# Part of a depthwise convolution moved from VectorE to ScalarE copies and GpSimd additions, in a two-layer hybrid block

## The chip, the core and the metric

The kernel runs on one core of a Trainium2 chip. The metric is the device time of one execution in microseconds, taken as the median over runs. The core has TensorE (PE in the profile, with its weight loads as PEld), VectorE (DVE), ScalarE (ACT), GpSimd (POOL) and SyncE (SP), which issues all DMAs here. Each engine works off its own instructions in order; the engines wait for each other by semaphores.

## The reference

Two layers of a block over 1024 latent tokens and 256 context tokens of width 1024. Each layer projects the normalised input into ten groups of columns and feeds three branches: a state-space branch (SSD) behind a convolution of 5 taps over 1280 channels, an attention branch, and a conformer branch:

```
def dwconv(x, w, b):
    pad = w.shape[0] // 2
    y = lax.conv_general_dilated(x, w[:, None, :].astype(x.dtype), ..., feature_group_count=x.shape[-1])
    return y + b.astype(x.dtype)
...
def conformer_branch(ua, ub, gate, conv_w, conv_b, ln_g, ln_b, pw_w, pw_b):
    u = ua * jax.nn.sigmoid(ub)
    u = jax.nn.silu(layernorm(dwconv(u, conv_w, conv_b), ln_g, ln_b))
    u = u @ pw_w + pw_b
    return u * jax.nn.silu(gate)
```

The conformer convolution is depthwise with 31 taps over 512 channels. The three branches are concatenated and multiplied by an output matrix; the result is gated and added to the input. In the second layer (layer 1 below) the context tokens get no output, so its convolution covers 1024 tokens and not 1280.

## The kernel before, in words

A layer has three stages that follow each other on TensorE: the projections (`phase_b`), attention with the SSD scan beside it (`attn`, `ssd`), and the output matrix (`out_half`). The program is written with a due time ahead of each group of instructions (`at(us)`); a scheduler that knows these times and a model of the engines makes from them one fixed order per engine. The order that results, and not the text of the code, is what runs.

The change lies in the second half of `phase_b`. It works through 17 blocks of 256 projected columns (`block`, numbered from 0 here). A block loads its weights as two halves, each in three steps: a DMA into a raw tile `wr` (L357, one buffer), a copy on ScalarE to the rounded part `wth`, a subtraction on GpSimd to the rest `wtl` (L359). Then come the matmuls, three for each of the eight slices of the depth (`wth` with the rounded input `hh`, `wtl` with `hh`, `wth` with the input's rest `hl`). The weight tiles have two buffers, so block i + 2 may be prepared once block i has been used. A block's output comes in groups of 512, 512 and 256 tokens of 24 matmuls each, in PSUM tiles `m` with four buffers, for each of its two halves.

Blocks 0 to 8 alternate. Even ones hold two of the ten 128-channel slices of the 5-tap convolution: ScalarE copies them into `xpad`, and `conv_x` computes `xcv` on VectorE with one tensor_scalar (L205), four scalar_tensor_tensor (L208), a tanh on ScalarE (`th`) and one more scalar_tensor_tensor. For eight of the ten slices TensorE then transposes `xcv` in three groups, and ScalarE copies those out into `xsg` (one buffer for all ten token tiles), which a single DMA stores. Odd blocks hold the gate `ub` and the value `ua` of one of four conformer slices j: VectorE forms `up` (two buffers, 15 zeros of padding written by GpSimd), and `conv_cm` computes slice j of the 31-tap convolution into `cac`, on VectorE alone: a tensor_scalar for tap 0 with the bias, then 30 scalar_tensor_tensor in place, each over 1295 elements per partition (1024 in layer 1), due 1.7 us apart (`CM_PACE`). I call these conv 0 to conv 3. Blocks 9 to 16 are gated projections (`z`, `gc`, `ga`), whose results go through ScalarE (`g_t`) and VectorE (`g_o`, two buffers) to memory.

`cm_tail` finishes the conformer branch: per token tile TensorE transposes the four `cac` slices, VectorE takes mean and variance (`bs`), normalises (`xn`), TensorE transposes back, and a small matrix product follows (`v`). Its due time is `TAIL` us after that of block 9's start, so its transposes come between the matmuls of blocks 9 to 16 in TensorE's order. A token tile's transposes need all four convolutions.

Of the kernel before, what the change touches and what calls it, by code (L numbers as in the profile page):

```python
# [10 lines left out]
AF = mybir.ActivationFunctionType  # L11
ALU = mybir.AluOpType
# [6 lines left out]
PT_ = 2  # L19
PX_ = 1  # L20
CM_PACE = 1.7
TAIL = 40.0
SSD_PACE = 25.0
AT_PACE = 1.2
VLAG = 1
# [13 lines left out]
NT = T // 128  # L39
# [121 lines left out]
def build(tc, a, out, depth=DEPTH, dump=None):  # L161
    nc = tc.nc
    es = ExitStack()
    V, S, G, P, Y = nc.vector, nc.scalar, nc.gpsimd, nc.tensor, nc.sync

    def at(us):
        tc.cur_priority = int(us * 100)

    def pool(st, name, bufs=1, **k):
        return st.enter_context(tc.tile_pool(name=name, bufs=bufs, **k))  # L170
# [3 lines left out]
    def mk(p, shape, tag, dt=F32, bufs=None):  # L174
        uid[0] += 1
        k = {} if bufs is None else {"bufs": bufs}
        return p.tile(shape, dt, tag=tag, name=f"{tag}_{uid[0]}", **k)
# [8 lines left out]
    def dr(shape, name, dt=F32):  # L186
        t = dp.tile(shape, dt, tag=name, name=name)
        if dump is not None:
            dump[name] = t
        return t  # L190
# [4 lines left out]
    def tr(o, i, idt):  # L195
        P.transpose(o, i, idt)  # L196

    def act(o, i, f, **k):
        S.activation(o, i, f, **k)  # L199

    def ts(e, o, i, s1, op0, s2=None, op1=None):
        if op1 is None:
            e.tensor_scalar(o, i, s1, None, op0)
        else:
            e.tensor_scalar(o, i, s1, s2, op0, op1)  # L205

    def stt(o, i, s, i1, op0, op1):
        V.scalar_tensor_tensor(o, i, s, i1, op0, op1)  # L208
# [24 lines left out]
    for l in range(depth):  # L233
        t = mk(cp, [128, NCOL], f"colc{l}")
        Y.dma_start(out=t, in_=a["colc"][l])
        colc.append(t)
        t = mk(cp, [128, NROW], f"rowc{l}")
# [18 lines left out]
    xt_d = dr([NT, 128, 768], "xt_d")  # L256
    bt_d = dr([NT, 128, 256], "bt_d")
# [11 lines left out]
    def rs_pow(o, i, scale, tmp, n):  # L269
        ts(V, tmp, i, scale, ALU.mult, EPS, ALU.add)  # L270
        G.tensor_tensor(o, tmp, neg[:, :n], ALU.pow)
# [38 lines left out]
    def cc(l, n, j=0, w=1):  # L310
        o = CO[n][0] + j * w
        return colc[l][:, o:o + w]
# [36 lines left out]
    def wblock(p, rp, src, tag, bufs, e=None, rtag="wr", rbufs=1):  # L349
        shape = list(src.shape)  # L350
        hi = mk(p, shape, tag + "h", F32R, bufs=bufs)
        lo = mk(p, shape, tag + "l", F32R, bufs=bufs)
        n = shape[1] // 2
        for k in range(2):
            s = slice(n * k, n * k + n)
            raw = mk(rp, [128, n, shape[2]], rtag, bufs=rbufs)
            Y.dma_start(out=raw, in_=src[:, s])  # L357
            act(hi[:, s], raw, AF.Copy)
            (e or G).tensor_tensor(lo[:, s], raw, hi[:, s].bitcast(F32), ALU.subtract)  # L359
        return hi, lo  # L360
# [73 lines left out]
    def phase_b(l, nh, b0, pp):  # L434
# [71 lines left out]
        gp = pool(st_r, f"gp{l}", side="right")  # L506
# [31 lines left out]
        up_p = pool(s2, f"up{l}")  # L538
        xp_p = pool(s2, f"xp{l}")
        cw = mk(up_p, [128, 4, 31], "cmw")  # L540
# [6 lines left out]
        NCM = 1024 if last else 1295  # L547

        def conv_cm(j, t0, pace):
            u, o = ups[j], cac[j]  # L550
            at(t0)
            ts(V, o[:, 0:NCM], u[:, 0:NCM], cw[:, j, 0:1], ALU.mult, cc(l, "cmb", j), ALU.add)
            for k in range(1, 31):
                at(t0 + k * pace)
                stt(o[:, 0:NCM], u[:, k:k + NCM], cw[:, j, k:k + 1], o[:, 0:NCM], ALU.mult, ALU.add)

        def conv_x(j, t0):
            xp = xps[j]
            at(t0)
            o = mk(xp_p, [128, 1282], "xcv", bufs=2)  # L560
            w = sw[:, 5 * j:5 * j + 5]
            ts(V, o, xp[:, 0:1282], w[:, 0:1], ALU.mult, sw[:, 50 + j:51 + j], ALU.add)
            for k in range(1, 5):
                at(t0 + 2 * k)
                stt(o, xp[:, k:k + 1282], w[:, k:k + 1], o, ALU.mult, ALU.add)
            at(t0 + 10)
            th = mk(up_p, [128, 1282], "th")
            act(th, o, AF.Tanh)
            stt(o, th, 1.0, o, ALU.add, ALU.mult)
            if j >= 6:  # L570
                d = bT_d[j - 6] if j < 8 else cT_d[j - 8]
                Y.dma_start(out=d[:, 0:1024], in_=o[:, 0:1024])
                Y.dma_start(out=d[:, 1024:1280], in_=o[:, 1026:1282])
            if j < 8:
                at(t0 + XLAG)
                sg = mk(gp, [128, NT, 128], "xsg")
                for ta in (0, 4, 8):
                    n = min(4, NT - ta)
                    ps = mk(*((pt, [128, 4, 128], "t") if ta == 4 else (px, [128, 4, 128], "x")))
                    for t in range(ta, ta + n):  # L580
                        c0 = t * 128 + (2 if t >= 8 else 0)
                        tr(ps[:, t - ta, :], o[:, c0:c0 + 128], idf)
                    act(sg[:, ta:ta + n, :], ps[:, 0:n, :], AF.Copy)
                if j < 6:
                    d = xt_d[:, :, 128 * j:128 * j + 128]
                else:
                    d = bt_d[:, :, 128 * (j - 6):128 * (j - 6) + 128]
                Y.dma_start(out=d.rearrange("t p f -> p t f"), in_=sg)

        def gate(ps, t0, n, d):  # L590
            th = mk(gp, [128, 512], "g_t", bufs=2)
# [59 lines left out]
        tlp = pool(s3, f"tl{l}")  # L651
# [4 lines left out]
        def cm_tail(c0):  # L656
            at(c0 - 10)
            pwh, pwl = wblock(tlp, wt, a["pww"][l], "pw", 1)
            hc = mk(tlp, [128, 16], "hc")
            ts(V, hc[:, 0:8], colc[l][:, CO["lng"][0]:CO["lng"][0] + 8], 0.5, ALU.mult)  # L660
            groups = [(0, 4), (4, 4)] + ([] if last else [(8, 2)])
            for tb, tn in groups:
                uh = mk(tlp, [128, 4, 512], "uh", F32R)
                ul = mk(tlp, [128, 4, 512], "ul", F32R)
                for t in range(tb, tb + tn):
                    at(c0 + 4 * t)
                    c1 = t * 128 + (15 if t >= 8 else 0)
                    ps = mk(pt, [128, 4, 128], "t")
                    for j in range(4):
                        tr(ps[:, j, :], cac[j][:, c1:c1 + 128], idf)  # L670
                    bs = mk(tlp, [128, 12], "bs", bufs=2)
                    V.bn_stats(bs[:, 0:6], ps.rearrange("p j t -> p (j t)"))
                    V.bn_aggr(bs[:, 6:8], bs[:, 0:6])
                    rs_pow(bs[:, 9:10], bs[:, 7:8], 1.0, bs[:, 8:9], 1)
                    xn = mk(gp, [128, 512], "xn", bufs=1)
                    ts(V, xn, ps.rearrange("p j t -> p (j t)"), bs[:, 6:7], ALU.subtract, bs[:, 9:10], ALU.mult)
                    ps2 = mk(px, [128, 4, 128], "x")
                    for j in range(4):
                        tr(ps2[:, j, :], xn[:, 128 * j:128 * j + 128], idf)
                    th = mk(tlp, [128, 4, 128], "lth", bufs=1)  # L680
                    v2 = mk(tlp, [128, 4, 128], "lv2", bufs=1)
                    for j in range(4):
                        g, b = hc[:, j:j + 1], hc[:, 4 + j:5 + j]
                        ts(V, v2[:, j], ps2[:, j], g, ALU.mult, b, ALU.add)
                    act(th, v2, AF.Tanh)
                    stt(v2, th, 1.0, v2, ALU.add, ALU.mult)
                    o = (t - tb) * 128
                    act(uh[:, :, o:o + 128], v2, AF.Copy)
                    G.tensor_tensor(ul[:, :, o:o + 128], v2, uh[:, :, o:o + 128].bitcast(F32), ALU.subtract)
                n = tn * 128  # L690
                at(c0 + 4 * (tb + tn))
                for f in range(4):
                    gcs = mk(gp, [128, 512], "gcs")
                    Y.dma_start(out=gcs[:, 0:n], in_=gc_d[f][:, tb * 128:tb * 128 + n])
                    ps = mk(pv_, [128, 512], "v")
                    pwx, ux = (pwh, pwl), (uh, ul)
                    mm3(ps[:, 0:n], lambda x, k: pwx[x][:, k, 128 * f:128 * f + 128],
                        lambda x, k: ux[x][:, k, 0:n], 4)
                    stt(gcs[:, 0:n], ps[:, 0:n], cc(l, "pwb", f), gcs[:, 0:n], ALU.add, ALU.mult)
                    ts(V, gcs[:, 0:n], gcs[:, 0:n], 0.5, ALU.mult)  # L700
                    Y.dma_start(out=yc_d[f][:, tb * 128:tb * 128 + n], in_=gcs[:, 0:n])
        cm_tail(g0 + TAIL)
        for i in range(14, 17):
            block(i)
# [481 lines left out]
    t0 = 35.0  # L1186
    at(12)
    nh = open_h(0)
    for l in range(depth):
        nh, t0 = layer(l, nh, t0)  # L1190
# [18 lines left out]
```

## Time and profile before

| what | value |
|---|---|
| time, median of 3 runs | 2921.86 us (2919.12 to 2928.43) |
| the profiled execution's own time | 2926.13 us |
| its span, first to last instruction | 2924.1 us |
| mean granted TensorE clock | 0.965 |
| busy: TensorE, VectorE | 2714.5 us, 2175.7 us |
| busy: GpSimd, ScalarE | 1165.6 us, 1062.2 us |

Durations come from the profiled execution. A row of the profile names the engine, the line of the kernel, the operation and the tiles as out<-in; behind a bar stand busy time and mean, then idle time of the engine before the operation and what ended it. Helpers issue most instructions, so L193 is any matmul, L196 any transpose, L199 any ScalarE operation, L205 any tensor_scalar and L208 any scalar_tensor_tensor: the tile's name tells which. In a tile's view the three durations are minimum, median and maximum in ns.

### The profile page before, as it was taken

How to read it: one execution, taken by the hardware profiler on the slowest of the kernel's cores; microseconds unless marked ns; L12 is line 12 of the kernel's file. 1: busy time of each engine (PE TensorE's matmuls, PEld its weight loads, DVE VectorE, ACT ScalarE, POOL GpSimd, SP SyncE). 2: the span in 40 equal slices, each digit the busy share in tenths (PEclk: the TensorE clock that was granted, in tenths of full speed). 3: DMA queues.
4: the chain of work that ended last, by engine and by line, in shares of the span. 5: the costliest groups of instructions: out<-in, count | busy, mean ns of one | idle time of the engine just before them, and what ended most of it. 6: DMA issues, size and time to landing. Idle time of an engine off the chain costs nothing. (4 is left out here: it accounts for less than half of the span.)

```text
span 2924.1 us, 41057 instructions
## 1 busy us (share of the span) xinstructions
PE 2714.5 (93%) x15708; PEld 2111.4 (72%) x15708; DVE 2175.7 (74%) x2987; ACT 1062.2 (36%) x1801; POOL 1165.6 (40%) x832
## 2 busy tenths in 40 slices
PE   5999998999998888999999999999998998999998
PEld 3888876888856655666787998877886665666676
DVE  4476899973299989797445587999835989898644
ACT  4212221222245454454335222222224454644432
POOL 2244122232168677571112352222323667675111
PEclk9999998999999989899999999999999999999999
DMA  6551111223343222224645322113234232312554
GB/s 237 191 159 66 56 55 65 90 98 105 115 137 108 73 88 84 74 68 130 205 147 162 114 76 67 55 63 107 102 127 151 73 98 72 103 59 62 164 152 143
DMA packets 284035, 314.44 MB, mean 108 GB/s; under 512 B 27606, under 2 KB 219190, under 8 KB 282814
## 3 DMA queue, kind: packets, MB, share of 16 engines
q1 hardware_dynamic: 283838, 311.82, 33.5%
q8 instruction: 123, 2.02, 0.3%
q14 instruction: 74, 0.61, 0.1%
HBM read 236.25 MB, written 75.50 MB: 107 GB/s over the span
## 5 line engine op out<-in xcount | busy, mean ns | idle before, releaser
L193 PE MATMUL m<-hh,wth 128*128 128x512 f32 (+1 forms) x1440 | 533.7, 371 | 0.1
L193 PE MATMUL m<-hl,wth 128*128 128x512 f32 (+1 forms) x1440 | 532.2, 370 | 0.0
L193 PE MATMUL m<-hh,wtl 128*128 128x512 f32 (+1 forms) x1440 | 531.6, 369 | 0.0
L199 ACT ACTIVATE a_p<-m 128x512 f32<-128x512 f32 x492 | 285.5, 596 | 373.1 <-PE m L193 362.7
L208 DVE SCALAR_TENSOR_TENSOR cac<-up,cmw,cac 128x1295 f32<-128x1295 f32 (+1 forms) x240 | 383.2, 1617 | 1.9
L935 DVE TENSOR_REDUCE a_sm<-m 128x1 f32<-128x512 f32 (+1 forms) x600 | 331.0, 583 | 52.8 <-PE m L193 50.2
L359 POOL TENSOR_TENSOR wtl<-wr,wth 128x1024 fp32r<-128x1024 f32 x68 | 201.9, 2969 | 404.2 <-ACT wth L199 404.1
L193 PEld LDWEIGHTS m<-hh,wth 128*128 128x128 f32 x1440 | 273.0, 190 | 47.8 <-ACT th L199 0.5
L193 PEld LDWEIGHTS m<-hh,wtl 128*128 128x128 f32 x1440 | 272.5, 189 | 48.1
L193 PEld LDWEIGHTS m<-hl,wth 128*128 128x128 f32 x1440 | 272.7, 189 | 47.3
L193 PE MATMUL m<-q_a,k_a 128*128 128x512 f32 (+1 forms) x656 | 255.3, 399 | 23.1 <-ACT a_p L199 10.9
L193 PE MATMUL m<-k_a,q_a 128*128 128x512 f32 (+1 forms) x600 | 242.0, 440 | 24.9 <-DVE a_sm L935 19.3
L193 PE MATMUL t<-a_p,vs 128*64 128x256 f32 x1968 | 250.9, 397 | 0.9 <-ACT a_p L199 0.4
L193 PE MATMUL m<-woh,yl 128*128 128x512 f32 x576 | 227.7, 397 | 6.1 <-DVE yl L1101 5.9
L193 PE MATMUL m<-woh,yh 128*128 128x512 f32 x576 | 226.6, 396 | 5.2 <-ACT yh L199 5.2
L193 PE MATMUL m<-wol,yh 128*128 128x512 f32 x576 | 226.6, 395 | 0.8 <-DVE wol L1077 0.8
L193 PE MATMUL m<-q_b,k_b 65*128 65x512 f32 (+1 forms) x656 | 223.1, 350 | 0.0
L193 PEld LDWEIGHTS t<-a_p,vs 128*64 128x64 f32 x1968 | 138.7, 142 | 89.1 <-issue 17.2
L193 PEld LDWEIGHTS m<-q_a,k_a 128*128 128x128 f32 x656 | 129.3, 197 | 84.3 <-ACT a_p L199 23.4
L193 PEld LDWEIGHTS m<-k_a,q_a 128*128 128x128 f32 x600 | 117.0, 201 | 99.6 <-DVE a_sm L935 38.2
L199 ACT ACTIVATE wth<-wr 128x1024 fp32r<-128x1024 f32 (+1 forms) x84 | 89.3, 1063 | 255.6 <-DMA wr<-in_wfm 136.2
L193 PE MATMUL m<-wth,hh 128*128 128x256 f32 (+1 forms) x608 | 173.6, 288 | 1.3 <-ACT wth L199 0.8
(239 smaller groups left out, 5629.5 us busy)
## 6 DMA issues: line engine op xcount, KB each, us to landing
wr<-in_wfm SPq DMA_DIRECT2D x68, 512.0 KB, 3.6
s_cb<-cum_d SPq DMA_DIRECT2D x72, 384.0 KB, 3.7
ada_w<-in_adaw SPq DMA_DIRECT2D x32, 512.0 KB, 4.6
wor<-in_wout SPq DMA_DIRECT2D x64, 256.0 KB, 3.1
s_x<-xt_d SPq DMA_DIRECT2D x38, 384.0 KB, 3.2
yf<-ys_d SPq DMA_DIRECT2D x36, 384.0 KB, 3.9
yf<-ya_d SPq DMA_DIRECT2D x36, 384.0 KB, 4.2
yf<-yc_d SPq DMA_DIRECT2D x36, 256.0 KB, 2.9
```

Source lines behind the costliest of these rows:

```text
L193: P.matmul(o, l, r, start=start, stop=stop)
L199: S.activation(o, i, f, **k)
L208: V.scalar_tensor_tensor(o, i, s, i1, op0, op1)
L359: (e or G).tensor_tensor(lo[:, s], raw, hi[:, s].bitcast(F32), ALU.subtract)
L935: V.tensor_reduce(sm[:, 2 * x + t, j:j + 1], ps[:, 0:kn], axis=AX.X, op=ALU.max)
```

## The change

```
-TAIL = 40.0
+TAIL = 20.0
+GTAPS = {0: 30, 2: 15}
...
         def conv_cm(j, t0, pace):
             u, o = ups[j], cac[j]
             at(t0)
-            ts(V, o[:, 0:NCM], u[:, 0:NCM], cw[:, j, 0:1], ALU.mult, cc(l, "cmb", j), ALU.add)
-            for k in range(1, 31):
+            nv = 31 - GTAPS.get(j, 0)
+            if nv > 1:
+                ts(V, o[:, 0:NCM], u[:, 0:NCM], cw[:, j, 0:1], ALU.mult, cc(l, "cmb", j), ALU.add)
+            else:
+                act(o[:, 0:NCM], u[:, 0:NCM], AF.Identity, scale=cw[:, j, 0:1], bias=cc(l, "cmb", j))
+            for k in range(1, nv):
                 at(t0 + k * pace)
                 stt(o[:, 0:NCM], u[:, k:k + NCM], cw[:, j, k:k + 1], o[:, 0:NCM], ALU.mult, ALU.add)
+            for k in range(nv, 31):
+                at(t0 + (nv - 1) * pace + (k - nv) * 2 * pace)
+                m = mk(up_p, [128, 1295], "cmt", bufs=2)
+                act(m[:, 0:NCM], u[:, k:k + NCM], AF.Copy, scale=cw[:, j, k:k + 1])
+                G.tensor_tensor(o[:, 0:NCM], o[:, 0:NCM], m[:, 0:NCM], ALU.add)
...
-                sg = mk(gp, [128, NT, 128], "xsg")
...
-                    act(sg[:, ta:ta + n, :], ps[:, 0:n, :], AF.Copy)
...
-                Y.dma_start(out=d.rearrange("t p f -> p t f"), in_=sg)
+                    sg = mk(gp, [128, 512], "g_o", bufs=2)[:, 0:128 * n].rearrange("p (t f) -> p t f", t=n)
+                    act(sg, ps[:, 0:n, :], AF.Copy)
+                    Y.dma_start(out=d[ta:ta + n].rearrange("t p f -> p t f"), in_=sg)
...
-                    xn = mk(gp, [128, 512], "xn", bufs=1)
+                    xn = mk(tlp, [128, 512], "xn", bufs=1)
...
-                    gcs = mk(gp, [128, 512], "gcs")
+                    gcs = mk(tlp, [128, 512], "gcs")
```

Conv 0 leaves VectorE whole: ScalarE writes tap 0 with the bias, and for each of the 30 other taps it writes a scaled copy into `cmt` (two buffers), which GpSimd adds to `cac` in place. Of conv 2 the last 15 taps go that way. Conv 1 and conv 3 stay as they were. `cm_tail` is due 20 us earlier. The transposed `xcv` are copied out and stored in three pieces, in the buffers `g_o` that the gates use later.

VectorE's order in layer 0, from the point where `up` of conv 0 is complete. Before, conv 0 (`cac_429`) starts at once, and `xcv` of the next block alternates with it:

```order
L208 SCALAR_TENSOR_TENSOR up_3094<-th_3015,m_3125 128x256
L205 TENSOR_SCALAR cac_429_2748<-up_3094,cmw_2744,colc_7_84 128x1295
L208 SCALAR_TENSOR_TENSOR cac_429_2748<-up_3094,cmw_2744,cac_429_2748 128x1295 x8
L205 TENSOR_SCALAR xcv_3274<-xpad_3217,scw_2745 128x1282
L208 SCALAR_TENSOR_TENSOR cac_429_2748<-up_3094,cmw_2744,cac_429_2748 128x1295
L208 SCALAR_TENSOR_TENSOR xcv_3274<-xpad_3217,scw_2745,xcv_3274 128x1282
```

Now:

```order
L209 SCALAR_TENSOR_TENSOR up_3102<-th_3023,m_3133 128x256
L206 TENSOR_SCALAR xcv_3342<-xpad_3285,scw_2745 128x1282
L209 SCALAR_TENSOR_TENSOR xcv_3342<-xpad_3285,scw_2745,xcv_3342 128x1282 x4
L209 SCALAR_TENSOR_TENSOR xcv_3342<-th_3348,xcv_3342 128x1282
L206 TENSOR_SCALAR xcv_3455<-xpad_3398,scw_2745 128x1282
L209 SCALAR_TENSOR_TENSOR xcv_3455<-xpad_3398,scw_2745,xcv_3455 128x1282 x4
L209 SCALAR_TENSOR_TENSOR xcv_3455<-th_3461,xcv_3455 128x1282
```

The two `xcv` of block 2 now stand right behind `up`, and the next convolution on VectorE is conv 1. Conv 3 (`cac_432`) is still the last of them in VectorE's order.

GpSimd's order at the same place, from block 2's weights on. Before, the two halves of each block's `wtl` stand side by side:

```order
L359 TENSOR_TENSOR wtl_3183<-wr_3188,wth_3182 128x1024
L614 MEMSET xpad_3326 128x2
L615 MEMSET xpad_3326 128x2
L616 MEMSET xpad_3326 128x2
L359 TENSOR_TENSOR wtl_3411<-wr_3412,wth_3410 128x1024
L359 TENSOR_TENSOR wtl_3411<-wr_3416,wth_3410 128x1024
```

Now:

```order
L360 TENSOR_TENSOR wtl_3251<-wr_3256,wth_3250 128x1024
L624 MEMSET xpad_3398 128x2
L625 MEMSET xpad_3398 128x2
L626 MEMSET xpad_3398 128x2
L360 TENSOR_TENSOR wtl_3487<-wr_3488,wth_3486 128x1024
L565 TENSOR_TENSOR cac_429_2748<-cac_429_2748,cmt_3160 128x1295
L565 TENSOR_TENSOR cac_429_2748<-cac_429_2748,cmt_3163 128x1295
L360 TENSOR_TENSOR wtl_3487<-wr_3492,wth_3486 128x1024
L565 TENSOR_TENSOR cac_429_2748<-cac_429_2748,cmt_3166 128x1295
```

Conv 0's additions stand between and behind the weight subtractions, some eight to a block up to block 6. Conv 2's 15 stand among those of blocks 9 and 10, all of them ahead of the `wtl` of block 11.

TensorE's order in layer 0 where the first transposes of conv 3 stand. `wth_5057` are the weights of block 11, `m_5127` is its third group. Before:

```order
L193 MATMUL m_5127<-hh_153,wtl_5058 128x256
L193 MATMUL m_5127<-hh_153,wth_5057 128x256
L196 MATMUL t_5641<-msk_74,cac_432_2751 128x128
L196 MATMUL t_5668<-msk_74,cac_432_2751 128x128
L193 MATMUL m_5127<-hl_154,wth_5057 128x256
```

Now, where `wth_4989` are the weights of block 10 and `m_5119` is its fifth group:

```order
L194 MATMUL m_5119<-hh_153,wth_4989 128x512
L194 MATMUL m_5119<-hl_154,wth_4989 128x512
L197 MATMUL t_5763<-msk_74,cac_432_2751 128x128
L197 MATMUL t_5790<-msk_74,cac_432_2751 128x128
L194 MATMUL m_5119<-hh_153,wtl_4990 128x512
```

The transposes stand 92 instructions further up in TensorE's order (row 2842, before it was 2934); in layer 1 it is 90 (row 8821, before it was 8911).

More of the change, by code (lines that the diff above doesn't have):

```diff
@@ L575, in conv_x @@
                 at(t0 + XLAG)
-                sg = mk(gp, [128, NT, 128], "xsg")
+                if j < 6:
+                    d = xt_d[:, :, 128 * j:128 * j + 128]
+                else:
+                    d = bt_d[:, :, 128 * (j - 6):128 * (j - 6) + 128]
                 for ta in (0, 4, 8):
@@ L582, in conv_x @@
                         tr(ps[:, t - ta, :], o[:, c0:c0 + 128], idf)
-                    act(sg[:, ta:ta + n, :], ps[:, 0:n, :], AF.Copy)
[L584 to L588, printed above, removed]
+                    sg = mk(gp, [128, 512], "g_o", bufs=2)[:, 0:128 * n].rearrange("p (t f) -> p t f", t=n)
+                    act(sg, ps[:, 0:n, :], AF.Copy)
+                    Y.dma_start(out=d[ta:ta + n].rearrange("t p f -> p t f"), in_=sg)
         def gate(ps, t0, n, d):
```

## Prediction

> **What bounds the kernel now.** I read the page's first part, then the busy times by stage.
>
> ```profile
> PE 2714.5 (93%) x15708; PEld 2111.4 (72%) x15708; DVE 2175.7 (74%) x2987; ACT 1062.2 (36%) x1801; POOL 1165.6 (40%) x832
> ```
>
> ```profile
> core 0: us, PE busy (x) PEld busy (x) DVE busy (x) ACT busy (x) POOL busy (x), PEclk, DMA share, GB/s
> 250.00:300.00 50.00, 50.00 (x269) 42.71 (x268) 28.48 (x24) 11.52 (x17) 11.02 (x18) 1.00 0.14 48
> 300.00:603.00 303.00, 278.45 (x1420) 234.93 (x1418) 297.92 (x193) 61.43 (x95) 69.33 (x43) 0.95 0.21 68
> 603.00:800.00 197.00, 194.39 (x1048) 165.72 (x1048) 76.11 (x157) 47.73 (x77) 44.96 (x31) 1.00 0.32 106
> 1754.00:1804.00 50.00, 50.00 (x243) 41.61 (x243) 32.41 (x31) 10.67 (x15) 15.26 (x19) 1.00 0.15 51
> 1804.00:2068.00 264.00, 251.62 (x1198) 207.44 (x1195) 262.90 (x188) 62.00 (x92) 64.06 (x42) 0.98 0.24 77
> 2068.00:2210.00 142.00, 141.32 (x639) 115.14 (x640) 63.27 (x114) 34.57 (x51) 38.57 (x26) 1.00 0.36 121
> ```
>
> Over the whole program TensorE carries the time. But 300 to 603 us (layer 0) and 1804 to 2068 us (layer 1), from the first conformer tap to the last, are VectorE's: it is busy for 297.9 of 303 us and 262.9 of 264 us. TensorE has gaps only there; just before and after it is full. The waits of TensorE say for whom (first layer 0, then layer 1):
>
> ```profile
> PE x L196 <- DVE xcv L208: 12.8, 2, 10.6
> PE x L196 <- ACT xsg L199: 5.4, 2, 5.0
> PE t L196 <- DVE xcv L208: 4.2, 1, 4.2
> PE t L196 <- DVE cac L208: 2.4, 1, 2.4
> ```
>
> ```profile
> PE t L196 <- DVE xcv L208: 11.7, 3, 6.1
> PE t L196 <- DVE cac L208: 1.3, 1, 1.3
> ```
>
> That is 24.8 and 13.0 us, 37.8 in all: this is what a lighter VectorE could give back, and hardly more. The last such wait is for conv 3 (`cac`), which ends each window. So the question is when conv 3 ends after the change.
>
> **Part 1: what leaves VectorE.** Per layer 30 taps and the opening tensor_scalar of conv 0, and 15 taps of conv 2: 45 taps and one tensor_scalar. The tile view of the two windows has their price:
>
> ```profile
> L208 DVE SCALAR_TENSOR_TENSOR cac<-up,cmw,cac x120: 1548/1556/3704, 300.6 to 601.6; 128x1295 f32<-128x1295 f32 x120
> L205 DVE TENSOR_SCALAR cac<-up,cmw,colc x4: 943/950/3031, 299.6 to 509.2; 128x1295 f32<-128x1295 f32 x4
> ```
>
> ```profile
> L208 DVE SCALAR_TENSOR_TENSOR cac<-up,cmw,cac x120: 1270/1275/3424, 1807.4 to 2065.2; 128x1024 f32<-128x1024 f32 x120
> L205 DVE TENSOR_SCALAR cac<-up,cmw,colc x4: 801/802/3041, 1804.4 to 1980.9; 128x1024 f32<-128x1024 f32 x4
> ```
>
> At the medians: 45 x 1.556 + 0.95 = 71.0 us in layer 0, 45 x 1.275 + 0.80 = 58.2 us in layer 1.
>
> **Part 2: what GpSimd's additions cost VectorE.** The maxima in those rows (3.70 and 3.42 us) are the clue. The timeline shows one of them, GpSimd's row first:
>
> ```profile
> 364.71 2.40 POOL L359 TENSOR_TENSOR wtl<-wr,wth 128x1024 fp32r<-128x1024 f32 x1 [14.63 <-ACT wth L199]
> ```
>
> ```profile
> 361.47 3.17 DVE L208 SCALAR_TENSOR_TENSOR cac<-up,cmw,cac 128x1295 f32<-128x1295 f32 x2
> 364.88 3.60 DVE L208 SCALAR_TENSOR_TENSOR cac<-up,cmw,cac 128x1295 f32<-128x1295 f32 x1
> ```
>
> Two taps alone take 3.17 us, 1.585 each. The tap beside GpSimd's subtraction takes 3.60: it stands still for 2.02 of the 2.40 us, a share of 0.84. So the two engines take turns on such operands, and the taps aren't moved to a free engine: they come back as standing time.
>
> The addition's own price: two rows of GpSimd adds from the attention stage.
>
> ```profile
> L974 POOL TENSOR_TENSOR a_ac<-a_p,a_p x24: 2358/2373/3350, 844.8 to 2720.8; 128x1024 f32<-128x1024 f32 x24
> ```
>
> ```profile
> L806 POOL TENSOR_TENSOR s_yo<-s_yo,s_of x34: 1806/1833/2859, 886.4 to 2677.5; 128x768 f32<-128x768 f32 x34
> ```
>
> 1024 elements cost 2.373 us, 256 more than 768 cost 0.540; 1295 elements so 2.373 + 271 x 0.540/256 = 2.945 us. Standing time at 0.84: 45 x 2.945 x 0.84 = 111.3 us in layer 0, 45 x 2.373 x 0.84 = 89.7 us in layer 1. Net on VectorE's window: +40.3 and +31.5 us. All 45 additions lie in it: GpSimd has done them before conv 2 is transposed, and conv 3 comes after that.
>
> The Trainium skill, page "SBUF — State Buffer", section "SBUF: two separate sides", says more: the port pair that VectorE and GpSimd share is an exclusive lock, held for the whole instruction, and a VectorE operation with two SBUF inputs counts. By that rule the share would be 1, not 0.84; the trace agrees with the turns, and the 2.02 of 2.40 us is what it shows of their length.
>
> **Part 3: TAIL 20 for 40.** TensorE reaches the transposes of conv 3 some 92 instructions earlier in layer 0 (row 2842 of its order for 2934) and 90 in layer 1 (8821 for 8911). If it waits there anyway, this work is left for after the wait. At 50.00/269 = 0.186 us and 50.00/243 = 0.206 us per matmul (the windows before): 17.1 and 18.5 us. After the window TensorE is full (194.4 of 197, 141.3 of 142), so nothing absorbs them.
>
> **Part 4: ScalarE's copies.** 46 per layer more, priced by its tanh of 1282 elements:
>
> ```profile
> L199 ACT ACTIVATE th<-xcv x8: 1262/1272/1285, 330.1 to 562.5; 128x1282 f32<-128x1282 f32 x8
> ```
>
> 46 x 1.27 = 58.4 us; ScalarE is busy for 61.4 of 303 us and hides them: zero on the path, at most 58 if its cover were gone. What queues behind them are the weights' copies (`wth`) and the PSUM evictions, by a copy or two.
>
> **Part 5: GpSimd's queue and the seams.** The weight subtractions `wtl` stand in GpSimd's order behind two to six additions. TensorE waits for them, and SyncE's loads of the next raw weights too. I don't count this beside part 2: while GpSimd works through its queue VectorE stands, and the other way round; the sum of the two is the window. It holds while one of the two has work. Where both wait for TensorE, the window grows. Those seams exist now:
>
> ```profile
> L208 DVE SCALAR_TENSOR_TENSOR up<-th,m 128x512 f32<-128x512 f32 x6 | 4.1, 684 | 3.4 <-PE m L193 3.4
> L208 DVE SCALAR_TENSOR_TENSOR up<-th,m 128x256 f32<-128x256 f32 x4 | 1.7, 419 | 4.0 <-PE m L193 4.0
> ```
>
> ```profile
> L208 DVE SCALAR_TENSOR_TENSOR up<-th,m 128x512 f32<-128x512 f32 x7 | 4.8, 681 | 4.9 <-PE m L193 4.9
> ```
>
> 7.4 and 4.9 us. With conv 2's buffer held until conv 0 has been read to its end I take as much again: +12.3. Bounds: none more (0), or a tenth of the new windows, (303 + 40 + 264 + 32)/10 = 64.
>
> **Part 6: pieces of transposed copies.** Three stores for one, 16 times: 32 issues more on SyncE.
>
> ```profile
> L588 SPq DMA_DIRECT2D xt_d<-xsg x12: 377/377/405, 299.2 to 1933.9; - x12
> ```
>
> 32 x 0.38 = 12 us of a queue over 567 us of windows, and nobody waits for them before the SSD stage: zero, at most 12. The gain is the 5.4 us wait on `xsg`; it is part of the 24.8 and goes, but VectorE's chain is what is late next. `xn` and `gcs` change pools, with one buffer as before: zero.
>
> **The sum.** 40.3 + 17.1 + 31.5 + 18.5 + 12.3 = +119.7 us. The profiled execution took 2926.1, so 3045.8 for such a one; it lay 4.3 above the median of the runs shown (2921.9): **3042** (3041.5). Its own range: below, no further seams (-12.3) and VectorE's `up`, which reads PSUM, all done inside additions (5.8 and 4.8 in the rows above, -10.6): 3019. Above, seams half way to their bound ((64 + 12.3)/2 = 38, +26): 3068.
>
> **Rivals.**
> - *The lock lasts the whole addition.* Share 1 for 0.84: 0.16 x 45 x (2.945 + 2.373) = +38.3: **3080**. For it: many additions will follow each other directly, with no free edge between. Against: the 0.84 of the row. The Trainium skill's page "SBUF — State Buffer" would have it so.
> - *Seams.* Both engines wait at block borders, since GpSimd's queue delays weights and thereby TensorE: +64 for +12.3: **3094**, with the whole lock 3132. For it: raw weights have a single buffer, which each `wtl` frees. Against: VectorE idles 5 us of 303 now.
> - *Milder turns.* Additions fall partly where VectorE doesn't need the operands: **2931 to 3019**, between the bound of a measurement below and the foot of the forecast's own range.
> - *Faster: the additions cost VectorE nothing.* Then its window shrinks by 71 and 58 us, TensorE's 37.8 us of waits go, and with them the lowered clock (0.95 and 0.98 in the windows; 0.05 x 303 + 0.02 x 264 = 20, half of it in the gaps already): 2921.9 - 37.8 - 10 = **2874**. It decides at a share where a layer breaks even: 45 x 2.945 x s + 17.1 = 71.0 gives s = 0.41; 45 x 2.373 x s + 18.5 = 58.2 gives 0.37. Below about 0.4 the change is no loss, at 0.84 it is one. For it: VectorE's operations that read PSUM (`up`, 0.68 us) are not stretched. Against: every stretched tap above.
>
> **How the numbers follow.** Forecast 0.42, whole lock 0.20, seams 0.15, milder turns 0.10, no change 0.04, faster 0.09. A measurement of this kernel tells about 0.3% (9 us). Slower by more: 0.42 + 0.20 + 0.15 + 0.10 = 0.87; within: 0.04; faster: 0.09. Range 2955 to 3150: it leaves out faster (0.09), no change (0.04), the mildest of the milder turns (0.03) and the worst seams (0.04).
>
> **What would show it.** Two groups of layer 0's window now:
>
> ```profile
> L208 DVE SCALAR_TENSOR_TENSOR cac<-up,cmw,cac 128x1295 f32<-128x1295 f32 x120 | 209.6, 1765 | 1.0
> ```
>
> ```profile
> L359 POOL TENSOR_TENSOR wtl<-wr,wth 128x1024 fp32r<-128x1024 f32 x19 | 68.0, 3580 | 179.1 <-ACT wth L199 179.1
> ```
>
> After, VectorE has 75 taps there and 40 operations on the eight `xcv`; the standing time of 45 additions and 19 `wtl` falls on them: (111.3 + 19 x 2.02)/115 = 1.30 us each, so taps average near 1.56 + 1.30 = 2.9 us for 1.77. The additions take 2.9 us at least and often over 4, as `wtl` takes 3.58 with its waits for 2.40. From the first use of conv 0 to conv 3's end layer 0 takes some 345 us, layer 1 some 295. TensorE's waits for `xcv`, `cac` and `wtl` rise from 25 to about 80 us in layer 0. The attention stage is as long as before. Wrong it is if taps stay near 1.6 us while additions run, or if conv 3 ends earlier than 303 us after the first tap.

## The result, and the profile after

The changed kernel takes 3061.4 us (median of 4 runs, 3060.0 to 3067.5), beside 2923.1 us for the kernel before on the same chip: a ratio of 1.0476, with a 95% interval of 1.0453 to 1.0498. It is slower by 138 us. The forecast was 3042 us, with a range of 2955 to 3150.

The profiled execution's span is 3058.2 us, 134.1 more than before. First the page's part 1, on busy time by engine:

```profile
PE 2730.7 (89%) x15708; PEld 2121.5 (69%) x15708; DVE 2199.0 (72%) x2895; ACT 1170.2 (38%) x1893; POOL 1479.1 (48%) x922
```

VectorE (DVE) runs 92 instructions fewer and is busy for 23 us more. The busy times by stage show where: the window of the conformer taps in layer 0, the stretch from there to the attention, and the same two in layer 1.

```profile
core 0: us, PE busy (x) PEld busy (x) DVE busy (x) ACT busy (x) POOL busy (x), PEclk, DMA share, GB/s
308.00:658.00 350.00, 265.62 (x1326) 223.11 (x1324) 310.22 (x144) 117.32 (x135) 239.95 (x87) 0.87 0.16 54
658.00:880.00 222.00, 216.19 (x1147) 183.68 (x1148) 78.72 (x161) 52.54 (x86) 48.91 (x34) 0.98 0.31 106
1886.00:2185.00 299.00, 238.78 (x1104) 195.43 (x1103) 273.38 (x138) 105.93 (x131) 198.52 (x85) 0.91 0.20 63
2185.00:2366.00 181.00, 175.34 (x786) 141.75 (x787) 61.98 (x122) 45.58 (x70) 45.89 (x30) 0.98 0.35 116
```

The windows grew from 303.6 to 350.5 us and from 264.3 to 298.5. VectorE is busier in them (297.9 to 310.2, 262.9 to 273.4), although 46 of its instructions (45 taps and a tensor_scalar) have left each. It also idles for 40 and 26 us there, where it had idled for 5 and 1. TensorE's granted clock falls to 0.87 and 0.91.

The two groups of layer 0 that the prediction named, and the additions between them:

```profile
L209 DVE SCALAR_TENSOR_TENSOR cac<-up,cmw,cac 128x1295 f32<-128x1295 f32 x75 | 190.7, 2550 | 0.9
L565 POOL TENSOR_TENSOR cac<-cac,cmt 128x1295 f32<-128x1295 f32 x45 | 173.5, 3855 | 18.2 <-ACT cmt L200 11.9 <-DVE cac L209 4.2
L360 POOL TENSOR_TENSOR wtl<-wr,wth 128x1024 fp32r<-128x1024 f32 x18 | 66.3, 3686 | 59.2 <-ACT wth L200 59.2
```

A tap had a mean of 1.765 us and now has 2.550; an addition has one of 3.855. The tile view tells how much of that is standing (minimum, median, maximum in ns):

```profile
L565 POOL TENSOR_TENSOR cac<-cac,cmt x45: 2925/4119/6738, 310.4 to 620.9; 128x1295 f32<-128x1295 f32 x45
L209 DVE SCALAR_TENSOR_TENSOR cac<-up,cmw,cac x75: 1551/1565/4290, 381.3 to 656.6; 128x1295 f32<-128x1295 f32 x75
```

Nine of the 45 additions met neither a `cac` nor an `xcv` instruction of VectorE, and each of them took 2.97 to 2.99 us, close to the 2.945 of the prediction. The median tap is as short as ever; others wait out an addition. TensorE's waits in layer 0 are 84.5 us for the 24.8 of before:

```profile
PE m L194 <- DVE g_o L209: 23.5, 2, 20.2
PE t L197 <- DVE xcv L209: 20.4, 2, 20.0
PE x L197 <- DVE xcv L209: 14.6, 1, 14.6
PE m L194 <- ACT th L200: 10.7, 1, 10.7
PE x L197 <- ACT g_o L200: 10.7, 1, 10.7
PE t L197 <- DVE cac L209: 4.6, 1, 4.6
```

Only the last row is conv 3's. The others are VectorE's gates and `xcv`, and ScalarE's tanh and copies, and they are spread over the whole window. In layer 1 the waits are 60.2 us for 13.0.

### The profile page after: what moved, and what is told of

It reads as the page before. It is cut to its first block, busy times and chain, and to the rows that moved or that the text cites. A ratio compares the mean times of both kernels' runs of the same rounds, so it can differ in the third digit from the quotient of the medians.

```text
span 3058.2 us, 41328 instructions
## 1 busy us (share of the span) xinstructions
PE 2730.7 (89%) x15708; PEld 2121.5 (69%) x15708; DVE 2199.0 (72%) x2895; ACT 1170.2 (38%) x1893; POOL 1479.1 (48%) x922
## 3 DMA queue, kind: packets, MB, share of 16 engines
q8 instruction: 123, 2.02, 0.3%
## 5 line engine op out<-in xcount | busy, mean ns | idle before, releaser
L194 PE MATMUL m<-hh,wth 128*128 128x512 f32 (+1 forms) x1440 | 541.0, 376 | 48.6 <-DVE g_o L209 24.0
L194 PE MATMUL m<-hh,wtl 128*128 128x512 f32 (+1 forms) x1440 | 538.3, 374 | 0.0
L200 ACT ACTIVATE a_p<-m 128x512 f32<-128x512 f32 x492 | 285.3, 595 | 363.9 <-PE m L194 355.1
L209 DVE SCALAR_TENSOR_TENSOR cac<-up,cmw,cac 128x1295 f32<-128x1295 f32 (+1 forms) x150 | 352.7, 2359 | 2.0
L565 POOL TENSOR_TENSOR cac<-cac,cmt 128x1295 f32<-128x1295 f32 (+1 forms) x90 | 316.0, 3511 | 21.4 <-ACT cmt L200 12.7
L360 POOL TENSOR_TENSOR wtl<-wr,wth 128x1024 fp32r<-128x1024 f32 x68 | 200.2, 2945 | 239.8 <-ACT wth L200 231.0
```

The source lines that it names most:

```text
L194: P.matmul(o, l, r, start=start, stop=stop)
L565: G.tensor_tensor(o[:, 0:NCM], o[:, 0:NCM], m[:, 0:NCM], ALU.add)
```

## The experiments

Each ratio is to the kernel before, on the same chip in the same session, with its 95% interval. The theory: GpSimd's additions read SBUF, and VectorE's taps stand still for most of an addition. The rivals: ScalarE's copies or the longer queues are the cost; the chain of additions in place is; the earlier place of conv 3's transposes is; the pieces and pools are.

**The additions left out.**

```
             act(m[:, 0:NCM], u[:, k:k + NCM], AF.Copy, scale=cw[:, j, k:k + 1])
-            G.tensor_tensor(o[:, 0:NCM], o[:, 0:NCM], m[:, 0:NCM], ALU.add)
```

> The change without its 90 GpSimd additions: ScalarE still writes the scaled copies, nobody adds them (45 taps per layer are left out of the result). Theory of turns (an addition on GpSimd stops VectorE's taps): VectorE's windows lose 71 and 58 us and nothing comes back, so TensorE's 37.8 us of waits go: about 2890 us. Rival, ScalarE's 92 copies cost the time (weights and evictions queue behind them): the time stays above 3000 us.

Measured: 2921.7 us, 0.9975 [0.9958, 0.9992]. The whole slowdown is gone with the additions; ScalarE's copies and the rest of the change cost nothing like it. But the gain that I expected of additions that cost nothing isn't there either. Layer 0's window without them:

```profile
L209 DVE SCALAR_TENSOR_TENSOR cac<-up,cmw,cac 128x1295 f32<-128x1295 f32 x75 | 138.1, 1851 | 0.9
L209 DVE SCALAR_TENSOR_TENSOR up<-th,m 128x512 f32<-128x512 f32 x6 | 4.1, 687 | 19.3 <-PE m L194 15.9 <-ACT th L200 3.4
```

```profile
308.00:580.00 272.00, 258.60 (x1331) 218.73 (x1329) 223.09 (x144) 115.78 (x136) 59.25 (x42) 0.97 0.22 69
```

VectorE is busy for only 223 of 272 us and waits for TensorE's `m` at `up`; TensorE is busy for 258.6 of 272 and bounds the window. The window is 31 us shorter than before, but TensorE has more left behind it (217.7 us to the attention, before 200.2). So the load that conv 0 and half of conv 2 put on VectorE was worth 13 us of this layer.

**GpSimd as busy, but without reading SBUF.** In place of each addition, three fills of the buffer that ScalarE wrote.

```
-            G.tensor_tensor(o[:, 0:NCM], o[:, 0:NCM], m[:, 0:NCM], ALU.add)
+            for _ in range(3):
+                G.memset(m[:, 0:NCM], 0.0)
```

> Each of the 90 GpSimd additions is replaced by three GpSimd memsets of the scaled copy, so GpSimd's queue stays about as full (and as much in the way of the weight subtractions), but GpSimd reads no operand from SBUF (the 45 taps per layer are left out of the result). Theory of turns: memsets don't stop VectorE, its taps stay near 1.55 and 1.28 us, about 2900 us. Rival, the full GpSimd queue delays the weights: TensorE waits as in the change, 3030 to 3060 us, with VectorE idle.

Measured: 2939.2 us, 1.0035 [1.0013, 1.0057]. Rows of the tile view, of the groups and of the window:

```profile
L566 POOL MEMSET cmt<- x135: 1170/1182/1867, 308.4 to 523.1; 128x1295 f32 x135
L200 ACT ACTIVATE cmt<-up,cmw x45: 1362/1377/1418, 307.0 to 517.3; 128x1295 f32<-128x1295 f32 x45
```

```profile
L209 DVE SCALAR_TENSOR_TENSOR cac<-up,cmw,cac 128x1295 f32<-128x1295 f32 x75 | 139.9, 1865 | 1.3
```

```profile
306.00:585.00 279.00, 260.46 (x1329) 219.21 (x1327) 232.96 (x144) 117.96 (x135) 211.90 (x177) 0.96 0.21 68
```

The first row is of the fills, the second of ScalarE's copies. Three fills take 3 x 1.18 = 3.55 us, longer than the 2.98 of an undisturbed addition, and GpSimd is busy for 212 of 279 us, in the change for 240 of 350: its queue is at least as full. The taps stay at the 1.85 us that they have without additions, and the window is 279 us for 350. The full queue isn't free: the ratio is 0.006 above that of the run without additions, and the 2900 us expected are missed. But the change is 0.050 above it, so the bulk of the cost isn't the full queue; it is GpSimd instructions that read SBUF. The Trainium skill's page "SBUF — State Buffer", section "SBUF: two separate sides", says just that: a VectorE operation with two SBUF inputs takes the shared port pair only against a GpSimd operation that reads SBUF. The 1.865 us beside fills and 2.550 beside additions agree.

**The additions without their chain.** Each adds to its own copy, and `cac` isn't touched.

```
-            G.tensor_tensor(o[:, 0:NCM], o[:, 0:NCM], m[:, 0:NCM], ALU.add)
+            G.tensor_tensor(m[:, 0:NCM], m[:, 0:NCM], u[:, k:k + NCM], ALU.add)
```

> The change with each GpSimd addition reading the scaled copy and up, and writing the scaled copy, in place of cac (the 45 taps per layer are left out of the result). GpSimd reads two operands from SBUF as in the change, but no result of VectorE or TensorE's transposes hang on the sum. Theory of turns: VectorE stands as in the change, 3030 to 3065 us. Rival, the memsets were cheap because the chain through cac was cut: 2920 to 2945 us as with the memsets.

Measured: 3051.2 us, 1.0430 [1.0414, 1.0446]. The groups of layer 0:

```profile
L209 DVE SCALAR_TENSOR_TENSOR cac<-up,cmw,cac 128x1295 f32<-128x1295 f32 x75 | 185.6, 2483 | 0.9
```

Nearly the whole cost is there without the chain through `cac` (the change: 1.0476, taps 2.550). That additions in place follow one another isn't what is slow.

**Additions of half the size.**

```
-            G.tensor_tensor(o[:, 0:NCM], o[:, 0:NCM], m[:, 0:NCM], ALU.add)
+            G.tensor_tensor(o[:, 0:NCM // 2], o[:, 0:NCM // 2], m[:, 0:NCM // 2], ALU.add)
```

> The change with each GpSimd addition over half of its elements (the other half of those 45 taps is left out of the result); GpSimd's and VectorE's orders stay nearly as in the change. Theory of turns: VectorE stands for half as long, so the time lies half way between the change (3061 us) and the change without additions (2922 us): 2980 to 3000 us. Rival, a fixed price per addition (an arbitration or an issue): 3040 to 3060 us.

Measured: 2967.1 us, 1.0127 [1.0100, 1.0154], below the 2980 to 3000 expected. Of the groups and the tile in layer 0:

```profile
L209 DVE SCALAR_TENSOR_TENSOR cac<-up,cmw,cac 128x1295 f32<-128x1295 f32 x75 | 151.8, 2032 | 0.9
```

```profile
L565 POOL TENSOR_TENSOR cac<-cac,cmt x45: 1570/1595/2851, 311.4 to 541.5; 128x647 f32<-128x647 f32 x45
```

From no additions to half ones the ratio rises by 0.015, from half to whole ones by 0.035. A fixed price per addition, the rival, is out. Nor is the cost proportional: 18 of the 45 half additions of layer 0 met neither `cac` nor `xcv` on VectorE, of the whole ones 9. Without additions VectorE idles for 49 of 272 us, and short additions fit into such gaps more often. That this is the whole reason is argued from these counts.

**TAIL back at 40.**

```
-TAIL = 20.0
+TAIL = 40.0
```

> The change with TAIL at 40 again. Theory: conv 3 ends as late as in the change, but TensorE has done 22 and 23 us more of matmuls by then; the gain is 36 to 45 us, about 3020 us. Rival, the place of the transposes doesn't matter because TensorE's waits lie at the xcv transposes: 3055 to 3065 us.

Measured: 3071.4 us (3059.9 to 3071.9), 1.0468 [1.0427, 1.0509]: the same as the change, and no 3020. The first transposes of conv 3 stay at row 2840 of TensorE's order, where the change has them at 2842 and the kernel before at 2934. Between 20 and 40 the due time doesn't set that place; the split of the taps does, since with the same 40 and all taps on VectorE (the run of the pieces alone, below) it is 2934 again. Presumably the scheduler's model has conv 3 end earlier when the taps are spread over two engines; that wasn't tested.

**TAIL at 80**, which moves them.

```
-TAIL = 20.0
+TAIL = 80.0
```

> The change with TAIL at 80: the first transposes of conv 3 now stand 205 instructions of TensorE later in layer 0 and 148 in layer 1, past the place that they have in the kernel before. The prediction's step (the work behind conv 3's end is lost time, since TensorE waits for it there): up to 205 x 0.186 + 148 x 0.206 = 69 us less, 2995 to 3025 us. Rival, TensorE's waits lie ahead of that place, at xcv, up and the gates, and only its 4.6 and 11.3 us at cac can go: 3045 to 3060 us.

Measured: 3052.6 us, 1.0426 [1.0405, 1.0447]. The transposes now stand at rows 3047 and 8969, 205 and 148 later than in the change. By the prediction's Part 3 that is 205 x 0.186 = 38 and 148 x 0.206 = 30 us less after the windows. There, the stretch from conv 3's end to the attention shrinks from 222.2 to 216.8 and from 181.5 to 174.7 us. The whole gains some 15 us by the two ratios (1.0476 - 1.0426; by the ends of the intervals 2 to 27). TensorE's longest waits in layer 0:

```profile
PE m L194 <- DVE g_o L209: 23.8, 2, 20.2
PE t L197 <- DVE xcv L209: 20.4, 2, 20.0
PE x L197 <- DVE xcv L209: 15.0, 1, 15.0
PE m L194 <- ACT th L200: 10.7, 1, 10.7
```

The wait for `cac` is gone (4.6 us in layer 0, 11.3 in layer 1, about what was gained), and the great ones stand as in the change. Conv 3's transposes are not where TensorE loses most of its time.

**The pieces and the pools alone**: all taps on VectorE, TAIL 40.

```
-TAIL = 20.0
-GTAPS = {0: 30, 2: 15}
+TAIL = 40.0
+GTAPS = {}
```

> Only the three pieces and the moved pools (all taps on VectorE, TAIL at 40). Theory: TensorE's wait of 5.4 us on the single store buffer goes, the 32 extra issues are hidden: 2915 to 2920 us. Rival, the pieces' shared buffers or the extra issues cost: 2928 us or more.

Measured: 2938.2 us, 1.0035 [1.0016, 1.0055]: this part isn't free, as I had put it. By stage it loses nothing in the windows (303.4 and 262.0 us, before 303.6 and 264.3). It is longer by 6.5 us ahead of the first conformer tap and by 14 between the two layers. The time of the first raw weight load differs, here that of before and then of this run:

```profile
91.04 0.33 SPq L357 DMA_DIRECT2D wr<-in_wtm  x1
```

```profile
96.50 0.33 SPq L358 DMA_DIRECT2D wr<-in_wtm  x1
```

In SyncE's order that load waits for other engines in the one and the other:

```
L357 DMA wr_945<-in_wtm 128x1024 [waits DVE_49,DMAHW0_49,Activation_49,Pool_49]
L358 DMA wr_945<-in_wtm 128x1024 [waits PE_49,DMAHW4_49,Activation_49,Pool_49]
```

Without `xsg`, `xn` and `gcs` the pool `gp` is smaller, so the buffers behind it move, and the raw weights come to lie on memory that TensorE still reads (in this program that of the tile `wkh`).

**The same pieces, with the pool as large as before.** `xn` and `gcs` go back to `gp`, and one tiny fill keeps a place for `xsg`.

```
+                if j == 0:
+                    G.memset(mk(gp, [128, NT, 128], "xsg")[:, 0, 0:2], 0.0)
...
-                    xn = mk(tlp, [128, 512], "xn", bufs=1)
+                    xn = mk(gp, [128, 512], "xn", bufs=1)
...
-                    gcs = mk(tlp, [128, 512], "gcs")
+                    gcs = mk(gp, [128, 512], "gcs")
```

> The pieces alone, with a tile of the old store buffer's size kept in the pool and the two other tiles in their old pool, so that the weight buffers lie where they lay before. Theory: the pieces cost nothing, but the smaller pool moves the first weight buffers onto memory that TensorE still reads, and they load later (8 us in layer 0, some 6 to 14 in layer 1): 2915 to 2922 us. Rival, the pieces themselves cost the 12 us that they showed: 2935 to 2940 us.

Measured: 2922.6 us, 0.9989 [0.9975, 1.0002], and the load's wait is that of before again. The stores in pieces cost nothing. The smaller pool costs the difference of the two ratios, 1.0035 - 0.9989 = 0.0046, or some 13 us (by the ends of the two intervals 4 to 23).

**The opposite of the change**: to the kernel before, the weight subtractions `wtl` of the first 12 blocks go from GpSimd to VectorE, although VectorE is what bounds the windows.

```
-            w = wblock(wt, wt, a["wfm"][l, i], "wt", 2)
+            w = wblock(wt, wt, a["wfm"][l, i], "wt", 2, V if i < 12 else None)
```

> The kernel before with the weight subtractions of blocks 0 to 11 on VectorE in place of GpSimd, the opposite of the change. Theory of turns: a subtraction on GpSimd stops VectorE for 2.02 us, on VectorE it takes about 1.25 us itself, so the windows shrink by 15 us each and TensorE's waits by some of that: 2900 to 2915 us. Rival without turns, VectorE gets 19 x 1.25 = 24 us more per window to do: 2950 us or more.

Measured: 2912.1 us, 0.9941 [0.9919, 0.9962]. The groups of VectorE and the window in layer 0:

```profile
L208 DVE SCALAR_TENSOR_TENSOR cac<-up,cmw,cac 128x1295 f32<-128x1295 f32 x120 | 189.2, 1593 | 0.9
L208 DVE SCALAR_TENSOR_TENSOR xcv<-xpad,scw,xcv 128x1282 f32<-128x1282 f32 x32 | 49.6, 1550 | 0.0
L359 DVE TENSOR_TENSOR wtl<-wr,wth 128x1024 fp32r<-128x1024 f32 x18 | 21.9, 1219 | 0.6 <-ACT wth L199 0.6
L208 DVE SCALAR_TENSOR_TENSOR xcv<-th,xcv 128x1282 f32<-128x1282 f32 x8 | 11.9, 1492 | 2.3 <-ACT th L199 2.3
L205 DVE TENSOR_SCALAR xcv<-xpad,scw 128x1282 f32<-128x1282 f32 x8 | 7.6, 946 | 0.5 <-ACT xpad L199 0.5
```

```profile
298.00:594.00 296.00, 284.02 (x1464) 240.03 (x1463) 285.30 (x214) 64.11 (x97) 6.18 (x26) 0.98 0.23 74
```

VectorE takes over 18 subtractions for 21.9 us and is busy for 285.3 us, 12.6 less than before, since its taps fall from 1.765 to 1.593 us. This version is 0.6% faster than the kernel before: little, but the whole interval lies below 1.

**That and the pieces together**, with the pool padded (the edits of the last two, TAIL 40, no taps moved).

> The kernel before with the weight subtractions of blocks 0 to 11 on VectorE, and the transposed copies in three pieces with the memory layout kept. Theory: the 14 us of the first, and some 3 to 5 us from the wait on the single store buffer: 2905 to 2912 us. Rival, the pieces add nothing once the windows are shorter: 2912 us as without them.

Measured: 2914.2 us, 0.9963 [0.9949, 0.9978]; `wtl` on VectorE alone is as good.

## Why the prediction was right, and where not

The sign, the mechanism and the size of the whole held: 134.1 us between the profiled spans, where the sum had 119.7. Its terms held less well, and that the total came so near is in part luck: Parts 2 and 5 erred by nearly the same in opposite directions, and Part 3 put 36 us on a step that failed.

**Part 1, what leaves VectorE** (-71.0, -58.2): 45 taps and a tensor_scalar a layer are gone, and the shortest taps cost what they did (1.551 us). It stands.

**Part 2, the standing time** (+111.3, +89.7): the mechanism is shown by four runs (no additions, fills, own additions, `wtl` moved). The size was too large. What stands in layer 0 shows in these groups of VectorE:

```profile
L209 DVE SCALAR_TENSOR_TENSOR xcv<-xpad,scw,xcv 128x1282 f32<-128x1282 f32 x32 | 72.8, 2275 | 0.4
L206 DVE TENSOR_SCALAR xcv<-xpad,scw 128x1282 f32<-128x1282 f32 x8 | 21.5, 2689 | 16.3 <-ACT xpad L200 16.3
L209 DVE SCALAR_TENSOR_TENSOR xcv<-th,xcv 128x1282 f32<-128x1282 f32 x8 | 17.9, 2239 | 2.7 <-ACT th L200 2.7
L209 DVE SCALAR_TENSOR_TENSOR up<-th,m 128x512 f32<-128x512 f32 x6 | 4.1, 682 | 14.9 <-PE m L194 14.2 <-ACT th L200 0.7
```

Against the means in the run with `wtl` on VectorE, where GpSimd hardly works (1.550, 0.946 and 1.492 us for these shapes; 1.556 is the old median of a tap): 75 x 0.99 + 32 x 0.73 + 8 x 1.74 + 8 x 0.75 = 118 us. The prediction had 111.3 for the additions and 19 x 2.02 = 38 for `wtl`, 149 together. About 30 us of it fell where VectorE had no such work: in the 40 us of idle time in the window, and beside `up`, which isn't stretched. The nine additions that met no `cac` and no `xcv` are 9 x 2.98 x 0.84 = 23 us of it. In this the rival *Milder turns* was right.

**Part 5, the seams** (+12.3): too small by about as much. VectorE's idle time rose by 35 us in layer 0 and 25 in layer 1, where I had 7.4 and 4.9; the 60 in all are near the 64 of the rival *Seams*. The rows above name it: `xcv` waits for `xpad` (16.3), `up` for TensorE's `m` (14.2), while TensorE's waits are for `g_o`, `th` and `xcv` of VectorE and ScalarE. The engines wait for each other in turn. But it isn't the seam that this rival named: TensorE has no wait for `wtl`, so it isn't weights delayed in GpSimd's queue that it stands for. Nothing in the working made the two errors cancel in the window, yet they do: busy +12.3 and idle +34.7 make the 47 measured, and the forecast had 40.3 + 7.4. In layer 1 they are +10.5 and +24.5, forecast 31.5 + 4.9.

**Part 3, TAIL** (+17.1, +18.5): the step failed. The transposes do stand earlier, but not through TAIL, and they aren't where TensorE loses its time: 205 and 148 rows later should have given 68 us and gave some 15, about its waits for `cac`. That the stretches after the windows are 22.0 and 23.1 us longer, near the figures of Part 3, doesn't bear it out: conv 3's end is a mark on VectorE, and what TensorE has left behind it depends on how late TensorE is by then. Without the additions it has 217.7 us left, with them 222.2. Only window and stretch together mean something: +68.9 us in layer 0, of which 59.7 are TensorE's waits, and +57.3 in layer 1, of which 47.2 are. Most of the rest is the clock: over window and stretch the same matmuls keep TensorE busy for 7.9 and 9.7 us longer, at a granted clock of 0.91 for 0.97 and of 0.94 for 0.98.

**Part 4, ScalarE's copies** (0): right. They take 1.38 us each (the `cmt` row beside the fills), ScalarE is busy for 117 of 350 us, and without the additions the same copies leave the kernel no slower than before.

**Part 6, pieces and pools** (0): right for the stores; wrong for the pools. "`xn` and `gcs` change pools, with one buffer as before: zero" overlooked that a smaller pool moves what is laid out behind it. That costs some 13 us, measured without the moved taps; the changed kernel itself is 8.0 us longer ahead of the first conformer tap and some 11 between the layers. The changed kernel with the old layout wasn't measured.

**The marks.** The window of layer 0 took 350.5 us (some 345 foretold), layer 1 298.5 (295), TensorE's waits 84.5 (80). Taps average 2.55 us for 2.9. The attention stages, foretold as unchanged, are some 6 us shorter each. Over all runs here they lie between some 554 and 563 us and between 492 and 500, without a link to any edit that I could find; that stays open.

**The rivals.** "The lock lasts the whole addition" isn't borne out, though it came nearer than the forecast had it. Four taps alternate with four additions in this stretch (GpSimd, then VectorE).

```profile
399.81 16.79 POOL L565 TENSOR_TENSOR cac<-cac,cmt 128x1295 f32<-128x1295 f32 x4
```

```profile
396.92 16.82 DVE L209 SCALAR_TENSOR_TENSOR cac<-up,cmw,cac 128x1295 f32<-128x1295 f32 x4
```

A tap takes 4.20 us, of which 1.585 are its own (two taps alone took 3.17): 2.62 standing of the 2.98 of an undisturbed addition, a share of 0.88, for the 0.84 of before. A share of 1 would make a pair 4.56 us. "Faster" had the wrong price too: on the same chip, and with the same small pool, the run without additions is 2938.2 - 2921.7 = 16.5 us below that of the pieces alone. So additions that cost nothing would bring some 17 us and not 48, since TensorE bounds next.

## What to carry to other kernels

Before work goes from VectorE to GpSimd, look in the trace for how VectorE's instructions stretch beside GpSimd's that read SBUF: where they met, VectorE stood for 0.84 to 0.88 of the GpSimd instruction's time. Moving a 1.56 us tap brought a 2.98 us addition in its place, so the move lost (4.8%) and its reverse won (0.6%). Ask also what bounds the stage once the busiest engine is relieved: here 71 us taken off VectorE in layer 0 were worth 13. And a tile that leaves a pool moves the buffers behind it: compare the waits of the first loads in the order of the queue.

## What the hardware showed that I had not expected

The turns between the two engines aren't always one for one. In the kernel before, a subtraction on GpSimd like the one of 2.40 us in the prediction takes 8.93:

```profile
459.01 8.93 POOL L359 TENSOR_TENSOR wtl<-wr,wth 128x1024 fp32r<-128x1024 f32 x1 [17.69 <-ACT wth L199]
```

VectorE in the meantime:

```profile
459.70 3.03 DVE L208 SCALAR_TENSOR_TENSOR cac<-up,cmw,cac 128x1295 f32<-128x1295 f32 x2
462.66 1.54 DVE L208 SCALAR_TENSOR_TENSOR xcv<-xpad,scw,xcv 128x1282 f32<-128x1282 f32 x1
464.13 1.55 DVE L208 SCALAR_TENSOR_TENSOR cac<-up,cmw,cac 128x1295 f32<-128x1295 f32 x1
465.60 3.03 DVE L205 TENSOR_SCALAR xcv<-xpad,scw 128x1282 f32<-128x1282 f32 x1
```

Four instructions of VectorE run unstretched while GpSimd stands, and only the fifth is held up. Here neighbours don't need each other's results, but that alone doesn't keep GpSimd out. In the changed kernel `cac` and `xcv` alternate too, and there each stands for a GpSimd instruction:

```profile
440.30 3.60 POOL L360 TENSOR_TENSOR wtl<-wr,wth 128x1024 fp32r<-128x1024 f32 x1
443.86 8.29 POOL L565 TENSOR_TENSOR cac<-cac,cmt 128x1295 f32<-128x1295 f32 x2
```

```profile
441.61 3.65 DVE L209 SCALAR_TENSOR_TENSOR cac<-up,cmw,cac 128x1295 f32<-128x1295 f32 x1
445.18 4.20 DVE L209 SCALAR_TENSOR_TENSOR xcv<-xpad,scw,xcv 128x1282 f32<-128x1282 f32 x1
449.30 4.21 DVE L209 SCALAR_TENSOR_TENSOR cac<-up,cmw,cac 128x1295 f32<-128x1295 f32 x1
```

What decides who goes next stays open.
